# A list scheduler's cost table: undisturbed durations, a shorter distance between engines, and one port that VectorE and GpSimd share

## The chip, the core and the metric

The kernel runs on one core of a Trainium2 chip. The metric is the device time of one execution in microseconds (us). Five engines matter here: TensorE (PE in the profile, with its weight loads as PEld), VectorE (DVE), ScalarE (ACT), GpSimd (POOL), and SyncE (SP), which issues the loads and stores.

## The reference, cut to what matters

One layer of a hybrid block runs over 1024 positions of width 1024, in float32:

```python
h = rmsnorm(x, norm_g)
q, k, v, z_a, u_b, v_b, z_b, g_a, g_b = split(h @ w_in)
y_a = stick_breaking_attention(q, k, v) * silu(z_a)      # 8 heads of 64, causal
y_b = spatial_gating(gelu(u_b), gelu(v_b), ...) * silu(z_b)
merged = sigmoid(g_a) * (y_a @ w_up_a) + sigmoid(g_b) * (y_b @ w_up_b)
out = rmsnorm(x + merged @ w_out, final_norm_g)
```

The attention weight of a key is a sigmoid times a running product over the later keys: a scan along the row.

## The kernel before

**Arithmetic.** Each float32 operand is split into a high part and a low part (`hi_lo`: ScalarE copies the high part, then VectorE or GpSimd subtracts it for the low part), and a product is three matmuls. The input projection runs as 18 groups (`project`), each made of seven products of 12 matmuls of 512 columns, with weight blocks added and subtracted first (Strassen's scheme). Tiles `a` hold raw weights, `b` their split parts, `T` the activations, and `X`, `Y`, `Z` are accumulators in PSUM.

**Attention.** For one block of 128 queries, `attn_row` makes the scores `z` on TensorE, two sigmoids on ScalarE (`keep` in tile `ak`, `beta` in tile `r`), a running product on VectorE (`scan`, line 198, on diagonal blocks; `scan_mult`, line 191, elsewhere), and `beta` times the scan on VectorE or GpSimd. `attn_step` then transposes the weights through TensorE into `tr`, splits them into two tiles `e`, and multiplies them by the values into `o`.

**Who runs what, and when.** Nothing is issued as it is written. Each helper of `Plan` (`mm`, `tt`, `scan`, ...) records a task with its engine, its cost in us, and what it depends on. `Plan.issue` then runs a list schedule: it keeps a clock, and whenever an engine is free it takes the ready task of lowest priority number whose tiles have slots (tiles of one tag are handed out in the order of their first use). A task is ready when its predecessors have ended, plus `LAT` where the predecessor is on another engine, plus 2.0 after a DMA; slots come free `LAT` after their last use. The result is one fixed order of instructions for each engine. On the chip each engine works through its order and waits at each instruction until its inputs are there; so costs and `LAT` change only the order. Which engine runs an operation is fixed in the code.

Priority is the order in which the code was written, except that weight preparation in `project` gets -9000 and groups written under `ahead` get -6000, on all engines but TensorE. TensorE thus takes the oldest work that the plan holds to be ready, and fills in with later products. The task that the plan takes is planned to end like this (line 284):

```python
pick.end = now + pick.cost
busy[eng] = pick.end
```

Planned costs before, for 512 columns: a VectorE `tensor_tensor` 0.841 with both inputs in SBUF and 0.683 with one in PSUM, a GpSimd one 1.530, a scan 1.446, a matmul 0.227.

Of the kernel before, what the change touches and what calls it, by code (L numbers as in the profile page):

```python
# [10 lines left out]
F32 = mybir.dt.float32  # L11
# [9 lines left out]
EPS = 1e-6  # L21
GELU_C = 0.044715
GELU_S = 1.5957691216057308
LAT = 0.7
SCAN = 2.0


class Buf:
# [14 lines left out]
    @property  # L43
    def all(self):
        return View(self, ())
# [38 lines left out]


class Task:
    __slots__ = ("eng", "cost", "fn", "bufs", "deps", "users", "idx", "prio", "tail", "waiting", "ready", "end")


class Plan:  # L90
# [13 lines left out]
    def add(self, eng, cost, fn, out, ins, tail=0.0):  # L104
        t = Task()
        t.eng, t.cost, t.fn, t.tail = eng, cost, fn, tail
        t.idx = len(self.tasks)
        t.prio = t.idx + (self.offset if eng != "PE" else 0)
        t.deps, t.users, t.bufs = set(), [], []
        for v, write in [(v, True) for v in out] + [(v, False) for v in ins]:  # L110
            b = v.buf
            for box, w, other in b.touched:
                if (w or write) and other is not t and all(a < d and c < e for (a, e), (c, d) in zip(box, v.box)):
                    t.deps.add(other)
            b.touched.append((v.box, write, t))
            if b.order is None:
                b.order = self.tag_count.get(b.tag, 0)
                self.tag_count[b.tag] = b.order + 1
            if b not in t.bufs:
                t.bufs.append(b)  # L120
                b.left += 1
        for o in t.deps:
            o.users.append(t)
        self.tasks.append(t)


    def mm(self, out, lhsT, rhs, start, stop, **kw):
        self.add("PE", max(0.109, rhs.n * 0.000417 + 0.0135),
                 lambda: self.nc.tensor.matmul(out.ap(), lhsT=lhsT.ap(), rhs=rhs.ap(), start=start, stop=stop, **kw),  # L129
                 [out], [lhsT, rhs])  # L130

# [30 lines left out]

    def tt(self, out, in0, in1, op, eng="DVE"):
        e = self.nc.vector if eng == "DVE" else self.nc.gpsimd
        near = in0.buf.psum or in1.buf.psum
        cost = out.n * (0.001042 if near else 0.00135) + 0.15 if eng == "DVE" else out.n * 0.00252 + 0.24
        self.add(eng, cost, lambda: e.tensor_tensor(out=out.ap(), in0=in0.ap(), in1=in1.ap(), op=op),  # L167
                 [out], [in0, in1])

# [17 lines left out]
                 [out], [in_])  # L187

    def scan_mult(self, out, in_, init=None):
        self.add("DVE", in_.n * 0.00255 + 0.14,  # L190
                 lambda: self.nc.vector.tensor_tensor_scan(out.ap(), in_.ap(), in_.ap(),  # L191
                                                           1.0 if init is None else init.ap(), op0=ALU.mult,
                                                           op1=ALU.bypass),
                 [out], [in_] + ([] if init is None else [init]))

    def scan(self, out, in_, floor, init):
        self.add("DVE", in_.n * 0.00255 + 0.14,
                 lambda: self.nc.vector.tensor_tensor_scan(out.ap(), in_.ap(), floor.ap(), init, op0=ALU.mult,  # L198
                                                           op1=ALU.max), [out], [in_, floor])

# [31 lines left out]


    def issue(self):
        now, seq = 0.0, 0
        events = []
        ready = {}
        busy = {}
        turn = {}
        free = dict(self.slots)  # L240
        order = []
        for t in self.tasks:
            t.waiting, t.ready = len(t.deps), 0.0
            busy.setdefault(t.eng, 0.0)
            ready.setdefault(t.eng, [])
            if not t.deps:
                heapq.heappush(ready[t.eng], (t.prio, t.idx, t))

        def can_start(t):
            need = {}  # L250
            for b in t.bufs:
                if not b.held:
                    need.setdefault(b.tag, []).append(b.order)
            for tag, orders in need.items():
                nxt = turn.get(tag, 0)
                if free[tag] < len(orders) or sorted(orders) != list(range(nxt, nxt + len(orders))):
                    return False
            return True

        done = 0  # L260
        while done < len(self.tasks):
            started = False
            for eng, heap in ready.items():
                if busy[eng] > now + 1e-9:
                    continue
                skipped = []
                pick = None
                while heap:
                    item = heapq.heappop(heap)
                    if can_start(item[2]):  # L270
                        pick = item[2]
                        break
                    skipped.append(item)
                for item in skipped:
                    heapq.heappush(heap, item)
                if pick is None:
                    continue
                for b in pick.bufs:
                    if not b.held:
                        b.held = True  # L280
                        free[b.tag] -= 1
                        turn[b.tag] = turn.get(b.tag, 0) + 1
                order.append(pick)
                pick.end = now + pick.cost
                busy[eng] = pick.end
                seq += 1
                heapq.heappush(events, (pick.end, seq, 0, pick))
                done += 1
                started = True
            if started:  # L290
                continue
            if not events:
                stuck = [(t.idx, t.eng, [(b.tag, b.order, b.held, turn.get(b.tag, 0), free[b.tag]) for b in t.bufs])
                         for h in ready.values() for _, _, t in sorted(h)[:4]]
                raise RuntimeError(f"no operation can start: {stuck[:12]}")
            now = events[0][0]
            while events and events[0][0] <= now + 1e-9:
                _, _, kind, t = heapq.heappop(events)
                if kind == 1:
                    heapq.heappush(ready[t.eng], (t.prio, t.idx, t))  # L300
                elif kind == 2:
                    free[t] += 1
                elif kind == 0:
                    for u in t.users:
                        lag = t.tail if t.eng == "DMA" else 0.0 if u.eng == t.eng else LAT
                        u.ready = max(u.ready, now + lag)
                        u.waiting -= 1
                        if u.waiting == 0:
                            seq += 1
                            heapq.heappush(events, (max(u.ready, now), seq, 1, u))  # L310
                    for b in t.bufs:
                        b.left -= 1
                        if b.left == 0 and b.tag in free:
                            seq += 1
                            heapq.heappush(events, (now + t.tail + LAT, seq, 2, b.tag))
        self.length = max(t.end for t in self.tasks)
        for t in order:
            ins = t.fn()
            if t.eng != "DMA":
                self.tc.keep_in_program_order(ins)  # L320
# [729 lines left out]
```

## Time and profile before

| what | value |
|---|---|
| time, median of 3 runs | 766.57 us (766.36 to 766.86) |
| the profiled execution: its time, its span | 766.53 us, 764.7 us |
| TensorE busy | 735.0 us (96% of the span), 3524 matmuls |
| VectorE busy | 575.0 us (75%) |
| ScalarE busy | 433.5 us (57%) |
| GpSimd busy | 308.8 us (40%) |
| granted TensorE clock, mean | 0.999 |

Busy time of an engine is the time in which at least one of its instructions was running. Matmuls are pipelined and their ends are modelled, so TensorE counts as busy a little past the point where the next matmul could have started. The span runs from the first to the last instruction; the execution's own time lies 1.8 us above it.

### The profile page before, as it was taken

How to read it: one execution, taken by the hardware profiler on the slowest of the kernel's cores; microseconds unless marked ns; L12 is line 12 of the kernel's file. 1: busy time of each engine (PE TensorE's matmuls, PEld its weight loads, DVE VectorE, ACT ScalarE, POOL GpSimd, SP SyncE). 2: the span in 40 equal slices, each digit the busy share in tenths (PEclk: the TensorE clock that was granted, in tenths of full speed). 3: DMA queues.
4: the chain of work that ended last, by engine and by line, in shares of the span. 5: the costliest groups of instructions: out<-in, count | busy, mean ns of one | idle time of the engine just before them, and what ended most of it. 6: DMA issues, size and time to landing. Idle time of an engine off the chain costs nothing.

```text
span 764.7 us, 10791 instructions
## 1 busy us (share of the span) xinstructions
PE 735.0 (96%) x3524; PEld 606.4 (79%) x3524; DVE 575.0 (75%) x788; ACT 433.5 (57%) x920; POOL 308.8 (40%) x298
## 2 busy tenths in 40 slices
PE   4989999999889999999999999999999999999996
PEld 3877788888777888887888888878888887888885
DVE  4868754688899787898999988897998878841122
ACT  6636474756756755666757676676867433411122
POOL 1500637497666576274345538234140300013110
PEclk9999999999999999999999999999999999999999
DMA  9412494424344375454543656354597677760022
GB/s 338 176 64 96 144 255 159 146 96 138 113 127 127 103 212 185 141 166 137 153 124 114 191 165 180 108 137 127 173 311 255 213 237 231 252 228 1 29 82 111
DMA packets 69177, 121.31 MB, mean 159 GB/s; under 512 B 7296, under 2 KB 17024, under 8 KB 69120
## 3 DMA queue, kind: packets, MB, share of 16 engines
q1 hardware_dynamic: 67968, 118.52, 49.3%
q10 hardware_dynamic: 1152, 2.10, 0.7%
q8 instruction: 28, 0.46, 0.3%
q14 instruction: 29, 0.24, 0.1%
HBM read 81.27 MB, written 39.32 MB: 158 GB/s over the span
## 4 chain that ended last, share of the span: by engine, by line
PE 83%; DVE 9%; issue 3%; DMA 2%; ACT 2%; POOL 1%; SPq 0%; POOLq 0%; DVEq 0%; ACTq 0%
PE Y L129 22%; PE X L129 21%; PE Z L129 18%; PE z L129 9%; PE o L129 8%; PE tr L133 5%; DVE b L167 2%; DVE ak L198 1%; DVE ak L191 1%; DMA k<-in_x_dram 1%; DVE e L167 1%; DMA k<-d 1%; DVE T L167 1%; DVE f L167 1%; DVE r L167 1%
## 5 line engine op out<-in xcount | busy, mean ns | idle before, releaser
L129 PE MATMUL Y<-T,b 128*128 128x512 f32 x672 | 180.0, 398 | 1.6 <-ACT b L157 1.3
L129 PE MATMUL X<-T,b 128*128 128x512 f32 x660 | 177.9, 398 | 0.0
L129 PE MATMUL Z<-T,b 128*128 128x512 f32 x540 | 145.2, 397 | 0.0
L129 PEld LDWEIGHTS Y<-T,b 128*128 128x128 f32 x672 | 122.3, 188 | 26.0 <-ACT b L157 1.7
L157 ACT CAST b<-a 128x512 fp32r<-128x512 f32 (+1 forms) x152 | 93.6, 617 | 81.9 <-PE Y L129 22.5
L129 PEld LDWEIGHTS X<-T,b 128*128 128x128 f32 x660 | 119.8, 188 | 22.8 <-POOL b L167 0.4
L167 DVE TENSOR_TENSOR b<-a,b 128x512 fp32r<-128x512 f32 (+1 forms) x112 | 99.4, 889 | 28.8 <-ACT b L157 20.0
L129 PEld LDWEIGHTS Z<-T,b 128*128 128x128 f32 x540 | 98.1, 188 | 18.3
L167 POOL TENSOR_TENSOR b<-a,b 128x512 fp32r<-128x512 f32 x40 | 60.7, 1516 | 119.8 <-ACT b L157 106.6
L198 DVE TENSOR_TENSOR_SCAN ak<-ak,c 128x128 f32<-128x128 f32 (+1 forms) x64 | 72.8, 1141 | 3.5 <-ACT ak L146 3.4
L167 POOL TENSOR_TENSOR a<-a,a 128x512 f32<-128x512 f32 x40 | 61.5, 1537 | 28.9 <-DVE b L167 15.3
L167 POOL TENSOR_TENSOR f<-f,f 128x512 f32<-128x512 f32 (+1 forms) x38 | 56.2, 1484 | 36.0 <-ACT f L146 14.7
L157 ACT CAST e<-tr 128x512 fp32r<-128x512 f32 (+1 forms) x96 | 45.7, 480 | 36.5 <-PE tr L133 33.3
L167 POOL TENSOR_TENSOR r<-r,ak 128x512 f32<-128x512 f32 x32 | 46.9, 1474 | 39.4 <-DVE ak L191 33.4
L133 PE MATMUL tr<-c,r 128*128 128x128 f32 x320 | 58.5, 273 | 2.6 <-DVE r L167 2.5
L129 PE MATMUL o<-e,k 128*128 128x512 f32 (+1 forms) x192 | 57.6, 343 | 3.3 <-DVE e L167 3.2
L146 ACT ACTIVATE ak<-z 128x128 f32<-128x128 f32 (+2 forms) x96 | 47.4, 494 | 20.4 <-PE z L129 18.1
L129 PE MATMUL z<-k,k 128*128 128x512 f32 (+2 forms) x216 | 56.8, 352 | 0.9 <-DMA k<-d 0.9
L167 DVE TENSOR_TENSOR e<-tr,e 128x512 fp32r<-128x512 f32 (+1 forms) x96 | 52.0, 545 | 7.3 <-ACT e L157 6.4
L146 ACT ACTIVATE r<-z 128x128 f32<-128x128 f32 (+2 forms) x96 | 46.9, 495 | 13.1 <-PE tr L133 12.5
L133 PEld LDWEIGHTS tr<-c,r 128*128 128x128 f32 x320 | 39.9, 140 | 13.6 <-DVE r L167 3.4
L191 DVE TENSOR_TENSOR_SCAN ak<-ak,c 128x512 f32<-128x512 f32 x32 | 50.5, 1588 | 0.2
(217 smaller groups left out, 1148.5 us busy)
## 6 DMA issues: line engine op xcount, KB each, us to landing
d<-f SPq DMA_DIRECT2D x112, 256.0 KB, 2.8
a<-in_w_pairs_dram SPq DMA_DIRECT2D x80, 256.0 KB, 2.8
f<-d SPq DMA_DIRECT2D x72, 256.0 KB, 3.2
k<-d SPq DMA_DIRECT2D x48, 256.0 KB, 4.8
k<-in_x_dram SPq DMA_DIRECT2D x8, 512.0 KB, 7.2
d<-b SPq DMA_DIRECT2D x16, 256.0 KB, 2.3
k<-d SPq DMA_DIRECT2D x8, 512.0 KB, 6.3
a<-in_w_up_dram SPq DMA_DIRECT2D x16, 256.0 KB, 4.3
```

Source lines behind the costliest of these rows:

```text
L129: lambda: self.nc.tensor.matmul(out.ap(), lhsT=lhsT.ap(), rhs=rhs.ap(), start=start, stop=stop, **kw),
L133: self.add("PE", 0.109, lambda: self.nc.tensor.transpose(out=out.ap(), in_=in_.ap(), identity=ident.ap()), [out], [in_, ident])
L146: return self.nc.scalar.activation(out=out.ap(), in_=in_.ap(), func=func, scale=sc, **kw)
L157: lambda: self.nc.scalar.copy(out=out.ap(), in_=in_.ap()), [out], [in_])
L167: self.add(eng, cost, lambda: e.tensor_tensor(out=out.ap(), in0=in0.ap(), in1=in1.ap(), op=op), [out], [in0, in1])
L191: lambda: self.nc.vector.tensor_tensor_scan(out.ap(), in_.ap(), in_.ap(), 1.0 if init is None else init.ap(), op0=ALU.mult, op1=ALU.bypass),
L198: lambda: self.nc.vector.tensor_tensor_scan(out.ap(), in_.ap(), floor.ap(), init, op0=ALU.mult, op1=ALU.max), [out], [in_, floor])
```

## The change

Four things in the cost table and one in the scheduler:

- `LAT`, the distance that the plan puts between engines and before a slot is reused, goes from 0.7 to 0.25 us.
- `tensor_tensor` costs go to 0.673 (VectorE) and 1.289 (GpSimd) for 512 columns, whatever memory the inputs lie in; scans go to 1.225.
- A matmul whose moving operand is float32 (not the rounded `float32r`) counts twice.
- A task of VectorE or GpSimd with more than one input view that is wider than 64 and lies in SBUF is marked `shared`. In the plan, shared tasks of both engines pass one port one after the other: a shared task ends at the later of now and the port's last end, plus its cost, and its engine is held until then.

```diff
-LAT = 0.7
+LAT = 0.25
...
+        t.shared = eng in ("DVE", "POOL") and len([v for v in ins if v.n > 64 and not v.buf.psum]) > 1
...
-        self.add("PE", max(0.109, rhs.n * 0.000417 + 0.0135),
+        self.add("PE", max(0.109, rhs.n * 0.000417 + 0.0135) * (2 if rhs.buf.dt == F32 else 1),
...
-        near = in0.buf.psum or in1.buf.psum
-        cost = out.n * (0.001042 if near else 0.00135) + 0.15 if eng == "DVE" else out.n * 0.00252 + 0.24
+        cost = out.n * 0.001042 + 0.14 if eng == "DVE" else out.n * 0.0024 + 0.06
...
-        self.add("DVE", in_.n * 0.00255 + 0.14,
+        self.add("DVE", in_.n * 0.0021 + 0.15,
...
-        now, seq = 0.0, 0
+        now, seq, port = 0.0, 0, 0.0
...
                 pick.end = now + pick.cost
+                if pick.shared:
+
+                    pick.end = port = max(now, port) + pick.cost
                 busy[eng] = pick.end
```

The scan's new cost stands in both `scan_mult` and `scan`. No instruction, tile, engine or buffer count is changed.

## Rows read from the trace of the kernel before

**Rows 1.** The page, part 1: busy time, share of span, instructions.
```profile
PE 735.0 (96%) x3524; PEld 606.4 (79%) x3524; DVE 575.0 (75%) x788; ACT 433.5 (57%) x920; POOL 308.8 (40%) x298
```
**Rows 2.** By stretch: length; PE, PEld, DVE, ACT, POOL busy; clock; DMA share, GB/s.
```profile
0.00:20.00 20.00, 8.83 (x32) 7.00 (x33) 9.92 (x19) 12.48 (x22) 3.07 (x12) 1.00 0.94 342
20.00:140.00 120.00, 116.40 (x529) 94.71 (x528) 80.10 (x122) 67.78 (x134) 47.00 (x39) 1.00 0.50 152
140.00:200.00 60.00, 60.00 (x296) 50.19 (x295) 47.17 (x66) 39.83 (x72) 41.49 (x34) 1.00 0.35 115
200.00:240.00 40.00, 35.27 (x167) 28.00 (x167) 39.30 (x44) 26.44 (x63) 29.28 (x24) 1.00 0.39 123
240.00:620.00 380.00, 377.52 (x1878) 312.68 (x1877) 333.15 (x435) 246.85 (x553) 169.70 (x167) 1.00 0.55 168
```
**Rows 3.** Waits of TensorE's matmuls, 140 to 620: total, times, longest.
```profile
PE o L129 <- DVE e L167: 3.2, 4, 1.5
PE tr L133 <- DVE r L167: 2.5, 2, 1.5
PE z L129 <- DMA k<-d: 0.9, 2, 0.7
PE o L129 <- DVE os L167: 0.5, 1, 0.5
```
**Rows 4.** Waits of TensorE's weight loads, 140 to 620.
```profile
PEld o L129 <- DVE e L167: 5.5, 6, 1.9
PEld tr L133 <- DVE r L167: 3.4, 2, 2.0
```
**Rows 5.** VectorE and GpSimd by tile: ns minimum/median/maximum, first and last start.
```profile
L167 DVE TENSOR_TENSOR b<-a,b x112: 410/687/1779, 70.2 to 597.6; 128x512 fp32r<-128x512 f32 x108, 128x256 fp32r<-128x256 f32 x4
L167 DVE TENSOR_TENSOR f<-Z,f x30: 659/692/694, 88.4 to 670.9; 128x512 f32<-128x512 f32 x30
L167 POOL TENSOR_TENSOR b<-a,b x40: 1284/1348/2321, 77.5 to 553.6; 128x512 fp32r<-128x512 f32 x40
L191 DVE TENSOR_TENSOR_SCAN ak<-ak,c x32: 1252/1339/2307, 231.8 to 611.3; 128x512 f32<-128x512 f32 x32
L167 DVE TENSOR_TENSOR r<-r,s x8: 682/1616/1791, 159.3 to 294.6; 128x512 f32<-128x512 f32 x8
```
**Rows 6.** Groups by line and shape: busy us, mean ns, idle before.
```profile
L191 DVE TENSOR_TENSOR_SCAN ak<-ak,c 128x512 f32<-128x512 f32 x32 | 50.5, 1588 | 0.2
L167 DVE TENSOR_TENSOR r<-r,s 128x512 f32<-128x512 f32 x8 | 11.8, 1478 | 0.3 <-POOL s L167 0.2
```
**Rows 7.** In order of time, near 347: start, length, instruction, idle before.
```profile
345.93 1.73 DVE L167 TENSOR_TENSOR b<-a,b 128x512 fp32r<-128x512 f32 x1
347.07 1.75 POOL L167 TENSOR_TENSOR b<-a,b 128x512 fp32r<-128x512 f32 x1
347.70 1.67 DVE L167 TENSOR_TENSOR a<-a,a 128x512 f32<-128x512 f32 x1
349.29 0.28 DVE L167 TENSOR_TENSOR e<-tr,e 128x128 fp32r<-128x128 f32 x1
349.62 0.33 PE L129 MATMUL o<-e,k 128*128 128x128 f32 x1 [0.83 <-DVE e L167]
```
**Rows 8.** In order of time, near 82.
```profile
82.30 1.98 PE L129 MATMUL Y<-T,b 128*128 128x512 f32 x8
82.50 0.59 ACT L157 CAST f<-X 128x512 fp32r<-128x512 f32 x1 [1.42 <-PE X L129]
```
**Rows 9.** In order of time, the start.
```profile
7.38 1.97 PE L133 MATMUL tr<-c,k 128*128 128x128 f32 x8 [7.38 <-DVE k L173]
9.19 1.06 ACT L146 ACTIVATE ak<-k 128x1024 bf16<-128x1024 f32 x1 [3.91 <-DMA k<-in_x_dram]
10.25 0.57 ACT L157 CAST T<-tr 128x512 fp32r<-128x512 f32 x1
14.05 1.16 ACT L157 CAST T<-a 128x512 fp32r<-128x512 f32 x2
```

More of the change, by code (lines that the diff above doesn't have):

```diff
@@ L86 @@
 class Task:
-    __slots__ = ("eng", "cost", "fn", "bufs", "deps", "users", "idx", "prio", "tail", "waiting", "ready", "end")
+    __slots__ = ("eng", "cost", "fn", "bufs", "deps", "users", "idx", "prio", "tail", "waiting", "ready", "end",
+                 "shared")
 class Plan:
@@ L196, in scan @@
     def scan(self, out, in_, floor, init):
-        self.add("DVE", in_.n * 0.00255 + 0.14,
+        self.add("DVE", in_.n * 0.0021 + 0.15,
                  lambda: self.nc.vector.tensor_tensor_scan(out.ap(), in_.ap(), floor.ap(), init, op0=ALU.mult,
```

## The prediction

> **What bounds the kernel now.** I read the page's busy times first. TensorE is busy for 735.0 of 764.7 us [rows 1], and the change adds and removes no instruction, so its work is the floor. All that another order can win lies in the 29.7 us in which TensorE is idle.
>
> The busy times by stretch say where those are [rows 2]. 11.2 us fall in the first 20 us (20.00 - 8.83), before and while the first blocks arrive; 3.6 between 20 and 140; none between 140 and 200; 4.73 in the forty microseconds from 200 to 240; 2.48 in the long stretch from 240 to 620; the other 7.7 after 620, most of them at the very end, where little choice of order is left. So the middle, 140 to 620, in which projections and attention are interleaved, holds 4.73 + 2.48 = 7.2 us. The reader is to see in the row of 200 to 240 that VectorE is busy for 39.30 of 40 us there: attention has begun, and TensorE waits for VectorE.
>
> The waits of TensorE's matmuls name the same thing: of 7.1 us between 140 and 620, 3.2 are waits of `o` for the low part `e`, 2.5 waits of a transpose for the weights `r`, 0.5 waits of `o` for an earlier output, and only 0.9 a DMA [rows 3]. VectorE ends 6.2 us of them. The weight loads, each of which counts as busy for a shorter time, give 5.5 + 3.4 = 8.9 us for the two large ones, against 5.7 by the matmuls [rows 4]. The true loss is between these.
>
> Why VectorE is late is seen in the durations [rows 5]. Its subtraction `b<-a,b`, both inputs in SBUF, takes 687 ns at the median and up to 1779; the same operation with one input in PSUM, `f<-Z,f`, never takes more than 694. GpSimd's takes 1284 at best and 2321 at worst. The timeline shows it at work [rows 7]: a VectorE subtraction of 1.73 us, a GpSimd one of 1.75 that overlaps it, a VectorE one of 1.67, each held by the other; behind them stands the 0.28 us `e` that TensorE has been waiting 0.83 us for. The two engines take turns, and the later one loses up to a whole operation of the other. The plan of before knows nothing of this: it charges 0.841 each time, right for the mean and wrong for nearly every single one, so the order it writes for TensorE puts attention steps where their inputs are not yet there.
>
> **The change, part by part.** The time is summed against the profiled execution's own 766.53 us, which is 0.04 below the median.
>
> *Durations and the port.* The new costs, 0.673 and 1.289, are the undisturbed ones (687 and 1284 ns [rows 5]), and the port adds the turn-taking where the plan sees it come. In the plan, then, a `z`, a transpose or an `o` becomes ready when it really does, and TensorE gets a product of `X`, `Y` or `Z` before it instead. Such products are at hand: weight preparation has the lowest priority numbers and runs ahead by several `b` tiles. What this can return is bounded by rows. At the low end it is 0: between 200 and 240 VectorE is busy 98% of the time, and if that is its own need, no order shortens it. At the high end it is the 6.2 us of waits for VectorE, or 9.4 (8.9 + 0.5) as the weight loads have it. I take half of the 6.2, so **-3.1 us**: in 240 to 620 VectorE is busy only 333 of 380 us, and the waits there are errors of order; in 200 to 240 part of the load is its own.
>
> *The shorter distance.* It costs no instruction, so its price is in order alone. Is 0.25 us true? After a matmul, ScalarE starts its copy at 82.50 where the next group's first matmul started at 82.30, so 0.20 us after the plan's end of the product [rows 8]. After VectorE, TensorE starts 0.05 us after the end (349.29 + 0.28 to 349.62) [rows 7]. So the new distance still lies above what the chip shows, where the old one lay 0.5 above. But this surplus was slack: an attention row passes from TensorE over ScalarE and VectorE back to TensorE, and loses 0.45 us of it per step. I cost it at **0** for the middle, because the named slack was needed against the blocks that the plan now counts; if the counting is wrong, the slack is missed (second rival). The shorter hold of slots is covered by the same argument.
>
> *The start.* Here a step moves, and I follow it through the plan's rules by hand, for the order alone. The second input block's square stands in ScalarE's order ahead of the first copy out of `tr`: it waits 3.91 us for the block's DMA until 9.19, and the copy comes at 10.25 [rows 9], though the transposes had begun at 7.38, eight of them taking 1.97. With four steps between engines each 0.45 us shorter, the plan has the first `tr` ready just before that block (7.55 against 7.92 on the plan's clock), so the copy goes first. On the chip it could then run at about 8.4. But the second and later copies still stand behind squares that wait for blocks; the first weights' copy at 14.05 ends this chain, and it can gain between 0 and one square (1.06). I take **-0.4**. Of the queues, SP's alone carries loads, and its order there keeps the order of the code; POOL's small operations behind the squares move with them.
>
> *Edits without effect.* The factor of two for float32 matmuls meets none: the moving operand of every `mm` (`T`, `e`, `kh`, `wv`, `ws`, `ys`, `wo`) is made as `float32r`, and transposes have their own cost. Nothing hides this; it is nothing.
>
> *What the port does not see.* `scan_mult` passes one wide view, since its two inputs are the same, and `wide(r)` in `r<-r,s` is 8 columns broadcast to 512; so neither is marked. Yet the rows show both held up: the scan at line 191 takes 1252 at best, 2307 at worst and 1588 on average, the product `r<-r,s` 682 at best and 1478 on average [rows 5, 6]. The plan charges 1.225 and 0.673. It thus lacks 32 x 0.363 + 8 x 0.805 = 18.1 us of VectorE time between 159 and 613; the old plan, charging 1.446 and 0.841, lacked 32 x 0.142 + 8 x 0.637 = 9.6. VectorE has 333 busy of 380 us there, so most of this is taken up by idle time; for the sum I leave it at 0, with a third of the 18.1, 6 us, as the other end. The Trainium skill, page "SBUF — State Buffer", section "Who interferes with whom", says that a VectorE instruction with two SBUF inputs contends with a GpSimd one that reads SBUF, and makes no exception for twice the same tile; by that rule the mark in this change is incomplete. The trace agrees: line 191 goes up to 2307 ns.
>
> The sum: 766.53 - 3.1 - 0.4 = **763.0 us**.
>
> **The rivals.**
>
> *Nothing reaches the end: 766.5.* The port itself is the limit where TensorE idles, and a better plan of a full queue is still a full queue. For it: 39.30 of 40 us [rows 2]. Waits move to other instructions and come to the same 7.2. Against it: after 240 VectorE has 12% to spare and TensorE still waits.
>
> *Slower: 769.* The unmarked operations, with the slack gone. Place: attention rows off the diagonal (line 191) and the normalisation (`r<-r,s`), 159 to 613. There the plan has VectorE ready too early by 18.1 us in all, and TensorE, in order, stands at a transpose or an `o` meanwhile. If a third reaches TensorE, the time is 766.5 - 3.5 + 6 = 769.0; if half, 772. It decides from 3.5 / 18.1, a fifth. For it: line 191 is 0.363 us over its planned cost on average. Against it: line 191 feeds GpSimd's product first, which is planned with the port, and TensorE mostly has products in between.
>
> *Much faster: 756 to 759.* All waits for VectorE go, as the weight loads count them, and the start gains a whole square: 766.5 - 9.4 - 1.06 = 756.1; with the matmuls' own count, 766.5 - 6.2 - 1.06 = 759.3. For it: between 140 and 200, with much GpSimd and VectorE work but before the first scans, TensorE has no idle time [rows 2]. Against it: the unmarked 18.1 us.
>
> **How the numbers follow.** The forecast (759.5 to 765.0) has 0.42, much faster 0.15, no change 0.20, slower 0.23. What this kernel's measurement can tell from no change is about 0.2%, or 1.5 us: below 765.0 is faster, above 768.1 slower. So faster is 0.57, same 0.20, slower 0.23. The range of 757.5 to 769.5 leaves out some 0.08 of the much faster end (unmarked blocks all harmless) and some 0.10 beyond the slower rival's first value. The forecast's own range is 759.5 to 765.0.
>
> **What will show it.** Right: between 200 and 240 TensorE is busy over 37 of 40 us, and its waits for `e` and `r` between 140 and 620 fall below 3.5 us, while its busy time stays at 735 or so. The maxima of `b<-a,b` stay near 1.78 us, since blocking is planned for, not removed. The copy out of `tr` comes before 9.19 at the start, and the first weights' copy before 14.05. Wrong: new waits of transposes behind line 191 or of `o` behind `e`, in the stretches after 240 (the slower rival); the same idle time between 200 and 240 with VectorE still at 98% (no change); or a gap near the end, should attention run out before the groups that fill its pauses.

## The result and the profile after

The changed kernel takes **785.23 us** (median of 4 runs, 784.01 to 786.99), the kernel before 766.70 beside it: **1.0244 times as long [1.0221, 1.0267]**, slower by 18.5 us. The forecast was 763.0, with a range that ended at 769.5. The profiled execution took 784.3 us with a span of 782.5, 17.8 above that of before.

The page's part 1 after, in the columns of [rows 1] (its span is 782.5 us):

```profile
PE 744.9 (95%) x3524; PEld 611.5 (78%) x3524; DVE 575.1 (73%) x788; ACT 433.3 (55%) x920; POOL 303.7 (39%) x298
```

The work of VectorE and ScalarE is the same to 0.2 us. TensorE, with the same 3524 matmuls, is busy 9.9 us longer; its mean granted clock is 0.987 in this execution, 0.999 before. By stretch, in the columns of [rows 2]:

```profile
0.00:20.00 20.00, 9.77 (x38) 7.73 (x39) 10.64 (x19) 12.05 (x22) 3.20 (x12) 1.00 0.91 328
20.00:140.00 120.00, 114.84 (x521) 93.73 (x521) 78.88 (x121) 68.31 (x136) 47.83 (x39) 1.00 0.48 151
140.00:200.00 60.00, 59.02 (x282) 48.68 (x282) 49.92 (x64) 37.52 (x68) 37.81 (x29) 1.00 0.34 113
200.00:240.00 40.00, 39.38 (x187) 32.52 (x186) 30.31 (x33) 20.94 (x45) 26.12 (x25) 1.00 0.41 140
240.00:260.00 20.00, 15.06 (x51) 10.87 (x50) 17.75 (x26) 13.79 (x34) 8.68 (x6) 0.67 0.33 85
260.00:640.00 380.00, 370.90 (x1832) 305.04 (x1832) 322.68 (x421) 241.45 (x542) 161.82 (x163) 1.00 0.53 161
```

Here it is better to count matmuls than busy time, since a matmul at a lower clock is busy longer for the same work. Before, 1878 of them ran in the 380 us from 240 to 620 [rows 2], one in 0.2023 us, 98.8 in 20 us. Against that rate, and stretch by stretch, after has 6 more before 20, 8 fewer from 20 to 140, 14 fewer from 140 to 200, 20 more from 200 to 240, 48 fewer from 240 to 260, and 46 fewer (1878 - 1832) in the 380 us from 260 to 640. Together some 90 matmuls are missing, 90 x 0.2023 = 18.2 us: about the whole difference of the spans, 17.8. The count is rough for single stretches, since it puts a transpose of 128 columns beside a product of 512: of the 51 in the gap 23 are transposes, so the work missing there is more than 48 mean matmuls, and the 14 fewer from 140 to 200, with 0.98 us of idle time, are in the main larger ones. So the forty microseconds that the prediction looked at did improve (idle 4.73 us before, 0.62 now), and the next twenty lost more than twice as much.

What TensorE does in those twenty is in the timeline (start, length, instruction, idle time before and what ended it):

```profile
240.03 0.40 PE L131 MATMUL Z<-T,b 128*128 128x512 f32 x1
242.09 0.50 PE L131 MATMUL o<-e,k 128*128 128x512 f32 x1 [1.24 <-ACT e L159]
243.77 1.11 PE L131 MATMUL o<-e,k 128*128 128x512 f32 x2 [1.18 <-DVE e L168]
246.59 1.48 PE L131 MATMUL z<-k,k 128*128 128x512 f32 x3
254.58 0.60 ACT L148 ACTIVATE r<-Y 128x512 f32<-128x512 f32 x1 [0.78 <-PE tr L135]
258.85 1.48 PE L131 MATMUL Y<-T,b 128*128 128x512 f32 x3
```

Between the last `Z` of one group at 240.03 and the first `Y` of the next at 258.85, its order holds attention alone: scores, transposes, outputs. Such a step goes round four engines, and with nothing else in the order TensorE waits out each round. The next group could not start its product because the accumulator `Y` was still held: the second spatial-gating group, `make_vb(1)`, reads its first quadrant out of `Y` into a tile `r` (254.58), slots of `r` are handed out in the order of first use, and the rows of the first head, `head(0, 0)`, are written before it and so come first. The scans show how late that head is. Its first scan stood at 203.1 before, and its first scan off the diagonal (line 191 before, 192 after) at 231.8 [rows 5]; they stand at 217.4 and 248.2 now, 14 and 16 us later, and the product behind them waits for attention's tiles:

```profile
L198 DVE TENSOR_TENSOR_SCAN ak<-ak,c x64: 409/972/2317, 203.1 to 598.4; 128x128 f32<-128x128 f32 x16, 128x256 f32<-128x256 f32 x16, 128x384 f32<-128x384 f32 x16, 128x512 f32<-128x512 f32 x16
L199 DVE TENSOR_TENSOR_SCAN ak<-ak,c x64: 405/1018/2308, 217.4 to 610.6; 128x128 f32<-128x128 f32 x16, 128x256 f32<-128x256 f32 x16, 128x384 f32<-128x384 f32 x16, 128x512 f32<-128x512 f32 x16
L192 DVE TENSOR_TENSOR_SCAN ak<-ak,c x32: 1257/1338/2417, 248.2 to 624.8; 128x512 f32<-128x512 f32 x32
```

The granted clock is lower there too. In the 20 us row it is 0.67; in five-microsecond stretches:

```profile
240.00:245.00 5.00, 2.58 (x9) 1.33 (x7) 4.86 (x9) 3.33 (x10) 1.30 (x2) 0.82 0.15 52
245.00:250.00 5.00, 5.00 (x20) 4.14 (x19) 4.50 (x8) 4.08 (x10) 0.34 (x1) 0.50 0.00 0
```

After two idle stretches of 1.24 and 1.18 us stands a fully busy row at 0.50, the lower level of 1.2 GHz, with 20 matmuls in 5 us. A part of TensorE's longer busy time is here.

The waits of TensorE's matmuls in the long stretch after the gap, 260 to 640, answer to [rows 3]:

```profile
PE z L131 <- DMA k<-d: 3.7, 3, 2.3
PE tr L135 <- POOL r L168: 2.0, 4, 1.0
```

There the waits for VectorE that the prediction wanted to shorten are nearly gone, and yet 46 matmuls are missing; the largest wait is now for a transfer of `k` (0.9 us in all before), the next one for the weights `r` that GpSimd multiplies.

### The profile page after: what moved, and what is told of

The parts are those of the page before. It is cut to its first block, busy times and chain, and to the rows that moved or that the text cites. A ratio compares the mean times of both kernels' runs of the same rounds, so it can differ in the third digit from the quotient of the medians.

```text
span 782.5 us, 10778 instructions
## 1 busy us (share of the span) xinstructions
PE 744.9 (95%) x3524; PEld 611.5 (78%) x3524; DVE 575.1 (73%) x788; ACT 433.3 (55%) x920; POOL 303.7 (39%) x298
## 4 chain that ended last, share of the span: by engine, by line
PE 73%; DMA 7%; DVE 7%; POOL 6%; issue 4%; ACT 2%; SPq 1%; POOLq 0%; DVEq 0%; ACTq 0%
PE Y L131 19%; PE X L131 17%; PE Z L131 15%; PE z L131 9%; PE o L131 8%; PE tr L135 4%; POOL r L168 3%; DMA f<-d 2%; DMA d<-f 2%; DVE r L168 1%; POOL b L168 1%; DVE b L168 1%; DMA k<-in_x_dram 1%; DVE f L168 1%; POOL a L168 1%
## 5 line engine op out<-in xcount | busy, mean ns | idle before, releaser
L131 PE MATMUL Y<-T,b 128*128 128x512 f32 x672 | 182.5, 402 | 3.5 <-ACT b L159 1.6
L131 PE MATMUL X<-T,b 128*128 128x512 f32 x660 | 174.2, 396 | 0.0
L131 PEld LDWEIGHTS X<-T,b 128*128 128x128 f32 x660 | 120.9, 188 | 22.7
L168 DVE TENSOR_TENSOR b<-a,b 128x512 fp32r<-128x512 f32 (+1 forms) x112 | 97.3, 870 | 42.3 <-ACT b L159 32.4
L168 POOL TENSOR_TENSOR b<-a,b 128x512 fp32r<-128x512 f32 x40 | 58.2, 1456 | 115.5 <-ACT b L159 99.1
L199 DVE TENSOR_TENSOR_SCAN ak<-ak,c 128x128 f32<-128x128 f32 (+1 forms) x64 | 69.5, 1091 | 0.3 <-ACT ak L148 0.2
L131 PE MATMUL o<-e,k 128*128 128x512 f32 (+1 forms) x192 | 63.5, 365 | 5.4 <-DVE e L168 2.5
L135 PE MATMUL tr<-c,r 128*128 128x128 f32 x320 | 63.0, 283 | 4.4 <-POOL r L168 3.3
L131 PE MATMUL z<-k,k 128*128 128x512 f32 (+2 forms) x216 | 60.7, 367 | 4.3 <-DMA k<-d 3.7
L135 PEld LDWEIGHTS tr<-c,r 128*128 128x128 f32 x320 | 42.6, 144 | 19.1 <-POOL r L168 6.6
L131 PEld LDWEIGHTS o<-e,k 128*128 128x128 f32 x192 | 37.7, 198 | 16.4 <-DVE e L168 4.9
```

Of the source, the lines that this page charges most:

```text
L135: self.add("PE", 0.109, lambda: self.nc.tensor.transpose(out=out.ap(), in_=in_.ap(), identity=ident.ap()), [out], [in_, ident])
```

## The experiments

Three theories stood at first. In the expectations, **theory 1** is that the port is the cause: a plan that serialises VectorE and GpSimd writes an order with a gap in it. **Theory 2** is that the shorter distance is the cause: 0.45 us of slack per step was needed, and without it TensorE stands at many small waits. **Theory 3** is that any new order moves the time by 1% or more, with no pattern. All ratios are to the kernel before, on the same chip. "The distance" is `LAT`.

### The four parts by themselves

**lat_only**: the kernel before with the short distance alone.

```diff
-LAT = 0.7
+LAT = 0.25
```

> The kernel before with the shorter distance alone (0.25 us), old costs, no port. Theory 1, the port: the 20 us with 51 matmuls come from the port in the plan, which makes attention's operations late there and lets projections run ahead; then this kernel has no such gap and takes 762 to 770 us. Theory 2, the lost slack: the shorter distance takes away what covered the blocks; then most of the loss is here, 778 us or more, as many small waits of transposes and of o. Theory 3, any new order: the time moves by 1% or more either way with no pattern over the four kernels.

**costs_only**: the changed kernel with the old distance and no port, so the new costs alone (with the factor for float32, which meets no matmul).

```diff
-LAT = 0.25
+LAT = 0.7
...
-                if pick.shared:
+                if False and pick.shared:
```

> The new costs alone: distance 0.7 us, no port. Theory 1: no long gap, 764 to 770 us. Theory 2: the slack is kept, so near the kernel before, 764 to 770 us too; it differs from theory 1 by what the next kernel does. Theory 3: anywhere from 760 to 785 us.

**no_port**: the changed kernel without the port.

```diff
-                if pick.shared:
+                if False and pick.shared:
```

> The changed kernel without the port: distance 0.25 us and new costs. Theory 1: the gap near 240 to 260 is gone and the time comes back to 765 to 772 us, with some small waits left because blocking is no longer counted. Theory 2: still slow, 778 us or more, since the distance is still 0.25 and costs are at their lowest. Theory 3: anywhere.

**port_lat70**: the changed kernel with the old distance.

```diff
-LAT = 0.25
+LAT = 0.7
```

> The changed kernel with the distance back at 0.7 us: new costs and the port. Theory 1: still slow, 780 us or more, since the longer distance makes the port's waits longer still in the plan and the gap stays. Theory 2: the slack is back, so 762 to 770 us. Theory 3: anywhere.

| kernel | distance | costs | port | us | ratio | plan's length | span |
|---|---|---|---|---|---|---|---|
| before | 0.7 | old | no | 767.12 | 1 | 758.0 | 764.7 |
| lat_only | 0.25 | old | no | 791.09 | 1.0316 [1.0301, 1.0332] | 757.2 | 788.6 |
| costs_only | 0.7 | new | no | 776.28 | 1.0128 [1.0113, 1.0143] | 754.3 | 774.3 |
| no_port | 0.25 | new | no | 807.91 | 1.0537 [1.0520, 1.0555] | 745.0 | 805.7 |
| port_lat70 | 0.7 | new | yes | 782.21 | 1.0202 [1.0186, 1.0217] | 779.9 | 780.2 |
| after | 0.25 | new | yes | 785.23 | 1.0244 [1.0221, 1.0267] | 760.5 | 782.5 |

The row of after is the result above, measured beside 766.70. The span is that of the profiled execution.

Every part makes the kernel slower by itself, and they don't add. The distance costs 24.0 us with the old costs (791.09 - 767.12), 31.6 with the new ones and no port (807.91 - 776.28), and only 3.0 with the port (785.23 - 782.21). The new costs alone take 9.2 us. The port takes 5.9 us more at the old distance, and *gives back* 22.7 at the short one (807.91 - 785.23). costs_only, which theories 1 and 2 both put at 764 to 770 us, missed both.

The plan's length is `Plan.issue`'s own (`self.length`): the end of its last task on its own clock. It is no measurement but follows from each kernel's code, and the order of matmuls that comes with it is the one in the trace. Set beside the span, it parts two losses. port_lat70's plan is 21.9 us longer than that of before, and the chip keeps to it (780.2 for 779.9): that loss is planned. no_port's plan is 13.0 us shorter, and the chip takes 60.7 us longer than the plan: that loss is the missing margin. The changed kernel has some of both. With the port, the short distance takes 19.4 us off the plan (779.9 to 760.5), and the chip returns none of it. Theory 3 does not fit: what the chip adds to the plan goes with the margin, 0.3 us with port and old distance, 6.7 before, 20.0 in costs_only, 22.0 after, 31.4 in lat_only, 60.7 with neither port nor old distance.

The traces show the two kinds. Without the port it is, in the main, many small waits. TensorE's, 140 to 640, lat_only:

```profile
PE o L129 <- DVE e L167: 9.7, 12, 2.1
PE o L129 <- ACT e L157: 7.5, 5, 3.5
PE tr L133 <- DVE r L167: 2.9, 5, 0.8
```

The same view of costs_only:

```profile
PE o L131 <- DVE e L168: 5.9, 9, 1.2
```

And of no_port:

```profile
PE o L131 <- DVE e L168: 23.0, 27, 1.8
PE o L131 <- ACT e L159: 5.9, 6, 2.3
PE tr L135 <- DVE r L168: 4.8, 7, 1.3
```

It is the wait of [rows 3], `o` for `e`, four times before, nine with costs_only, 12 with lat_only and 27 with both: each step towards a more hopeful plan puts more `o` where their `e` isn't there yet. (The view also counts the `o` of the gating groups, which reads a tile `b`; attention's alone, `o<-e,k`, are 4, 7, 8 and 21.)

But lat_only has a long gap too, without the port. From 280 to 300 TensorE gets through 53 matmuls, 46 below the mean rate, some 9.3 of the 24.0 us; the longest wait in it is not attention's but the second gating group's:

```profile
280.00:300.00 20.00, 13.17 (x53) 9.71 (x52) 14.92 (x19) 8.99 (x16) 15.45 (x13) 0.79 0.53 175
292.45 0.58 PE L129 MATMUL o<-e,b 128*128 128x256 f32 x1 [3.53 <-ACT e L157]
```

This gap is in the plan: lat_only's plan leaves TensorE idle for 10.4 of the 40 us from 260 to 300, that of before for none.

With the port the loss is a few long stretches. port_lat70 by stretch:

```profile
160.00:200.00 40.00, 34.56 (x164) 27.98 (x163) 31.45 (x40) 19.18 (x38) 27.87 (x26) 0.91 0.33 105
240.00:280.00 40.00, 34.88 (x154) 27.76 (x153) 32.08 (x39) 22.79 (x47) 21.63 (x15) 0.87 0.27 81
```

Against 198 matmuls in 40 us, the first row lacks 34 and the second 44: 78 x 0.2023 = 15.8 us, about the whole of its 15.1 us. Its plan holds both: TensorE is planned for 31.6 of the 40 us from 160 to 200, and for 26.2 of those from 240 to 280. The two gaps are of different kinds. In the second, attention is alone, as in the changed kernel. The first lies before any attention (the first scan is at 196.6); its longest wait is the first gating group's:

```profile
180.39 0.58 PE L131 MATMUL o<-e,b 128*128 128x256 f32 x1 [3.69 <-ACT e L159]
```

So both theories hold in the main, each in its own place: theory 1 for what the change does with the port, theory 2 for the distance without it.

### Where the distance matters

**margin_into_pe**: the kernel before, with 0.25 everywhere but where TensorE is the one that waits.

```diff
-    lag = t.tail if t.eng == "DMA" else 0.0 if u.eng == t.eng else LAT
+    lag = t.tail if t.eng == "DMA" else 0.0 if u.eng == t.eng else 0.7 if u.eng == "PE" else 0.25
...
-    heapq.heappush(events, (now + t.tail + LAT, seq, 2, b.tag))
+    heapq.heappush(events, (now + t.tail + 0.25, seq, 2, b.tag))
```

> The kernel before (old costs, no port) with the distance at 0.25 us everywhere, for slots too, but 0.7 us where TensorE is the one that waits. Theory 4: the distance is a margin for the bottleneck alone; TensorE must not be sent to an attention step early, the other engines may. Then this returns most of the 24 us that 0.25 us everywhere cost: 766 to 772 us, with TensorE's waits for e at some 4 us. Theory 5: each engine works in order, so a ScalarE or VectorE instruction that is sent early holds up those behind it, and the margin counts on every hop: 780 us or more.

779.91 us, 1.0163 [1.0133, 1.0193]: of lat_only's 3.16% about half comes back. That is far from theory 4's 766 to 772 and at the edge of theory 5's 780. The margin that counts is not only the one on the last step into TensorE; the rest must lie in the steps among the other engines, through which TensorE is reached, and in the slots, which the next run prices. Its waits, 140 to 640, are spread over every producer:

```profile
PE o L129 <- ACT e L157: 4.1, 3, 2.5
PE tr L133 <- DVE r L167: 3.0, 4, 1.3
PE tr L133 <- POOL r L167: 2.3, 2, 1.9
PE o L129 <- DVE e L167: 2.3, 4, 1.0
```

**slots_only**: the kernel before, with 0.25 for the release of slots alone (the second pair of lines above).

```diff
-    heapq.heappush(events, (now + t.tail + LAT, seq, 2, b.tag))
+    heapq.heappush(events, (now + t.tail + 0.25, seq, 2, b.tag))
```

> The kernel before with only the slots' release at 0.25 us after the last use, the distance between engines still 0.7. Theories 4 and 5 both: slots are freed by semaphores as fast as data, so little changes: 764 to 770 us. If the shorter hold of slots is what hurt, 778 us or more.

769.82 us, 1.0034 [1.0015, 1.0052]. As both theories had it, the release of slots matters little: by itself it costs 2.6 us.

### What the slack is slack against

**no_reads** puts a constant fill in the place of GpSimd's wide operations with two inputs, in the order of before, so that GpSimd reads nothing wide from SBUF; **no_reads_lat25** does the same in the order of lat_only.

```diff
+        if eng == "POOL" and out.n > 64:
+            o = out.f32() if out.buf.dt == F32R else out
+            self.add(eng, cost, lambda: e.memset(o.ap(), 0.5), [out], [in0, in1])
+            return
```

> The kernel before, in its own order, but each of GpSimd's wide tensor_tensor is replaced by a memset of the same output (the values computed are left out; it reads nothing, so VectorE should not be held up). VectorE's b<-a,b should then stay at 0.69 us throughout. Theory 6: TensorE's waits for VectorE come from the blocks; they all but vanish, 755 to 762 us. Theory 7: they come from the order itself; 763 us or more.

> The same replacement in the kernel with the distance alone at 0.25 us, which took 24 us longer than before. Theory 6: the margin of 0.7 us covers the blocks, and without blocks 0.25 us is enough: within 6 us of the run with the same replacement and 0.7 us. Theory 7: the margin covers other errors of the plan; still 15 us or more behind it.

756.86 us, 0.9863 [0.9842, 0.9884], and 764.27 us, 0.9959 [0.9945, 0.9972]. no_reads by tile:

```profile
L171 DVE TENSOR_TENSOR b<-a,b x112: 420/691/695, 70.0 to 587.8; 128x512 fp32r<-128x512 f32 x108, 128x256 fp32r<-128x256 f32 x4
L169 POOL MEMSET b<- x40: 519/527/530, 73.2 to 542.6; 128x512 f32 x40
L195 DVE TENSOR_TENSOR_SCAN ak<-ak,c x32: 1259/1276/1285, 224.5 to 601.5; 128x512 f32<-128x512 f32 x32
```

The longest `b<-a,b` falls from 1779 ns [rows 5] to 695 and the longest scan from 2307 to 1285, so nearly all of the variation in these durations was GpSimd's reading. No order was changed, and TensorE's idle time in 200 to 240 is gone:

```profile
200.00:240.00 40.00, 40.00 (x200) 33.33 (x199) 31.02 (x52) 29.13 (x69) 9.93 (x25) 1.00 0.48 148
```

This answers a question that [rows 2] left open: of VectorE's 39.30 us there, at least 8 were waiting and not need, since more instructions (52 for 44) now take 31.02. Without GpSimd's reads, the short distance costs 7.4 us in place of 24.0. Some 16.6 of the 24 us were therefore the blocks; the recorded expectations had set within 6 and 15 or more as the two answers, and the result lies between, nearer to the blocks. The 7.4 have one place, the planned gap of lat_only's order, which no_reads_lat25 shares. By stretch:

```profile
260.00:300.00 40.00, 34.44 (x161) 28.01 (x160) 25.17 (x42) 19.42 (x41) 10.13 (x23) 0.87 0.56 181
```

37 of 198 matmuls are missing in this row, 37 x 0.2023 = 7.5 us. Without blocks the chip keeps near the plan at either distance: spans of 754.8 and 762.4 us for plans of 758.0 and 757.2. One reservation on the 16.6: a fill takes 527 ns where the subtraction took 1284 or more [rows 5], so GpSimd itself is also less late, and they hold that as well.

The Trainium skill, page "SBUF — State Buffer", section "Who interferes with whom", says that GpSimd instructions which only write SBUF do not contend with VectorE's second input. These two runs agree: with fills in the place of GpSimd's wide operations, no subtraction `b<-a,b` took above 695 ns.

### A fuller port

**marked_all**: the changed kernel, with the operations marked too that the prediction found unmarked, the wide scan and `r<-r,s`.

```diff
+        self.tasks[-1].shared = True
...
             pl.tt(t3, t3, wide(r), ALU.mult)
+            pl.tasks[-1].shared = True
```

> The changed kernel with the two unmarked operations marked as shared as well (the scan with the same tile twice, and the product with a column broadcast). Rival of the prediction, unmarked operations: the waits after 260 are theirs, so TensorE's idle time from 260 to 640 falls from 9 us to 4 or less, and the time goes to 780 us or below, unless the plan itself puts a new gap in. Theory 1 turned round, the plan's own gaps: a fuller port delays attention further in the plan, more idle time is planned, and the time rises to 788 us or more with one or two long gaps.

801.82 us, 1.0447 [1.0423, 1.0471]: a plan that knows more of the blocks is some 16 us slower still, and the plan itself is 783.0 us long, 22.5 longer than that of the changed kernel. The rows by stretch show a second gap of the first one's kind:

```profile
240.00:260.00 20.00, 12.95 (x48) 8.50 (x49) 17.91 (x26) 12.94 (x34) 9.21 (x6) 0.79 0.33 86
640.00:660.00 20.00, 13.54 (x51) 8.35 (x51) 19.69 (x28) 11.65 (x32) 7.79 (x5) 0.78 0.06 19
```

VectorE is busy for 17.91 and 19.69 of 20 us in them. The slower rival, that the unmarked operations are the price, is not borne out: to mark them returns nothing. In the changed kernel itself, 260 to 640, TensorE waits for no `r` of VectorE's and for 2.0 us of GpSimd's, which is made from the scan; even if all of it were the scan's, it is a small part of 18.5 us.

### The gap itself

**free_accumulator**: the changed kernel, with the second gating group's first quadrant copied out of PSUM into a tile `f2`, whose slots don't stand behind the head's.

```diff
-        after(0, 0, xx.all, True)
+        if g == VB[1]:
+            c11 = buf("f2")
+            pl.copy(c11.all, xx.all)
+            after(0, 0, c11.all, False)
+        else:
+            after(0, 0, xx.all, True)
```

> The changed kernel with one ScalarE copy more: in the second spatial-gating group the first quadrant is copied out of PSUM, so that its accumulator is free without a tile r. If the gap of 240 to 260 is there because the next group's first product waits for this accumulator, which waits for attention's turn in r, the products of Y come before 250 and the gap there goes; the time falls to 770 to 775 us if nothing else holds them, or stays at 783 to 790 us with the gap moved to the next place where attention has to be finished. If the accumulator is not the cause, the gap stays at 240 to 260.

789.57 us, 1.0282 [1.0253, 1.0310]. By stretch:

```profile
240.00:260.00 20.00, 20.00 (x99) 16.52 (x98) 14.68 (x23) 12.77 (x33) 6.68 (x6) 1.00 0.30 88
260.00:300.00 40.00, 29.07 (x111) 21.40 (x110) 30.05 (x41) 22.05 (x42) 24.02 (x19) 0.74 0.37 110
```

The gap leaves 240 to 260 (99 matmuls in place of 51) and stands from 260 to 300, where 87 of 198 are missing. The held accumulator was what ended the products at 240, as read; it was not the cause of the loss. Products spent earlier are missing later: as read, attention, which is late, still has its rows to go round.

**head_first_lat70** and **head_first_lat25** act on that, in port_lat70 and in the changed kernel. They change three priorities at once: the first head's rows go ahead of all weight preparation, the first gating group's weight preparation goes back to its place in the code, and so does the second `u` group, which ran ahead.

```diff
+        self.pe_offset = 0
-        t.prio = t.idx + (self.offset if eng != "PE" else 0)
+        t.prio = t.idx + (self.offset if eng != "PE" else self.pe_offset)
...
+        prep = 0 if g == VB[0] else -9000
-        use_at, pl.offset = pl.offset, -9000
+        use_at, pl.offset = pl.offset, prep
...
-            pl.offset = -9000
+            pl.offset = prep
...
+    pl.offset, pl.pe_offset = -9500, -800
     head(0, 0)
-    ahead(make_u, 1)
+    pl.offset = pl.pe_offset = 0
+    make_u(1)
```

> New costs, the port and the distance of 0.7 us (782.2 us as it stood), with three priorities changed: the first attention head ahead of all weight preparation, the first spatial-gating group's preparation and the second u group at their place in the code. Theory 1 turned round: the loss with port and 0.7 us is idle time that the plan itself holds where attention begins; if attention starts first, the plan holds 17 us less of it, and the chip follows the plan: 763 to 767 us. If the chip does not follow, 775 us or more.

> The same three priorities in the changed kernel (distance 0.25 us). The gap of 240 to 260 goes or shrinks to half, and the many small waits stay, since the margin is still short: 775 to 783 us. If the small waits were a consequence of the late start too, 770 us or less.

772.28 us, 1.0061 [1.0043, 1.0080], where port_lat70 had 782.21; and 777.07 us, 1.0136 [1.0113, 1.0159], where the changed kernel has 785.23. By stretch, head_first_lat70:

```profile
160.00:200.00 40.00, 38.35 (x194) 31.79 (x193) 33.73 (x45) 23.56 (x45) 28.00 (x25) 1.00 0.35 112
200.00:240.00 40.00, 36.97 (x182) 29.40 (x182) 38.17 (x49) 27.66 (x64) 24.43 (x20) 1.00 0.35 102
240.00:280.00 40.00, 40.00 (x195) 33.23 (x194) 34.15 (x44) 25.51 (x46) 29.86 (x23) 1.00 0.52 157
```

And head_first_lat25:

```profile
200.00:240.00 40.00, 37.02 (x174) 30.02 (x173) 33.89 (x47) 26.27 (x61) 20.40 (x16) 0.91 0.28 82
240.00:260.00 20.00, 20.00 (x93) 16.54 (x93) 13.04 (x19) 13.36 (x23) 13.77 (x12) 1.00 0.55 174
260.00:640.00 380.00, 371.53 (x1831) 306.15 (x1830) 322.53 (x418) 236.64 (x534) 164.11 (x162) 1.00 0.54 165
```

The long gaps are gone in head_first_lat70, and in head_first_lat25 the one from 240 to 260; there a shorter one remains from 200 to 240, with 174 matmuls and a clock of 0.91. The first scan off the diagonal now stands at 213.8 and 209.8. That gives back about 10 and 8 us. So these priorities make the gaps. Which of the three does it was not separated: the lateness of the first head fits the gap from 240 on, and the first gap of port_lat70, before attention, can't be its work. Between 260 and 640, head_first_lat25 has 1831 matmuls where the changed kernel has 1832: taking the gap away returned nothing there. The first result is between its two recorded answers (763 to 767, or 775 and more), the second as expected. No version with the port, the new costs or the short distance was faster than before.

## Why the prediction was wrong, by its steps

**Durations and the port, forecast -3.1: the step that failed, and by most.** At the old distance these parts cost 15.1 us (782.21 against 767.12), 9.2 by the costs and 5.9 by the port. The reading of the loss was right: the waits were blocks, a plan that counts them moves TensorE's waits elsewhere, and in 200 to 240 TensorE is busy for 39.38 us where over 37 was foretold. What failed is the cover, "such products are at hand", and with it the floor of 0: a new order can lose. With the port the plan has less of VectorE and GpSimd to hand out, and the first head gets through its rows later, whatever the distance: its first scan off the diagonal stands at 231.8 before, 248.2 after and 248.3 in port_lat70, and without the port at 224.3 in no_port.

```profile
L192 DVE TENSOR_TENSOR_SCAN ak<-ak,c x32: 1253/1277/2243, 248.3 to 634.1; 128x512 f32<-128x512 f32 x32
```

So products are spent early, and at 240 attention stands alone. The gain of 4.1 us came, and 9.7 us (48 matmuls) went in the next 20. That weight preparation at -9000 takes VectorE and GpSimd first is read from the priorities and not shown by itself. All this could be had before the run: the plan of the changed kernel has TensorE at work for 10.8 of the 20 us from 240 to 260, that of before for all 20. The prediction followed the plan's rules by hand at the start alone and argued for the middle.

**The shorter distance, forecast 0: the second error.** Beside the port, as the prediction priced it, it costs 3.0 us; by itself 24.0. It was priced at 0 on the argument that the slack was needed against blocks which the plan now counts. The runs support the first half (without GpSimd's reads 7.4 us in place of 24.0, and those 7.4 in one planned gap) and the second in part (3.0 us with the port, 31.6 without). Yet the 19.4 us that the short distance takes off the plan with the port never reach the chip. The 0.20 and 0.05 us of distance [rows 7, 8] said only what an undisturbed step takes. The prediction set no other end to this term, although it named the 0.45 us that each step loses.

**Port and distance together.** At the old distance the port is a loss of 5.9 us, at the short one a gain of 22.7. It works as a substitute for slack and is the poorer one. Slack lets the order absorb any delay; the port moves only those that the plan foresees, and pays in planned idle time (754.3 us of plan without it, 779.9 with it, at the old distance). The new costs alone cost 9.2 us: the old 0.841 had been slack of another kind. The prediction calls it right for the mean; the mean of the subtraction was 0.887, so it lay 46 ns too low, and the new 0.673 lies 214 ns too low:

```profile
L167 DVE TENSOR_TENSOR b<-a,b 128x512 fp32r<-128x512 f32 x108 | 95.7, 887 | 26.3 <-ACT b L157 17.5 <-PE Z L129 3.7 <-POOL b L167 3.2
```

**The start, forecast -0.4: right, and mis-sized.** In order of time, as [rows 9]:

```profile
8.38 0.58 ACT L159 CAST T<-tr 128x512 fp32r<-128x512 f32 x1 [3.22 <-PE tr L135]
8.97 1.06 ACT L148 ACTIVATE ak<-k 128x1024 bf16<-128x1024 f32 x1
13.13 1.14 ACT L159 CAST T<-a 128x512 fp32r<-128x512 f32 x2
```

The copy goes ahead of the square, at the 8.4 foretold, and the weights' copy comes 0.92 us earlier (14.05 to 13.13), near the other end of 1.06. TensorE's idle time in the first 20 us falls from 11.17 to 10.23. But from 20 to 140 it rises from 3.60 to 5.16, so by 140 the gain is gone; the prediction took it as kept to the end.

**Maxima of `b<-a,b`: right.** They stay, since blocks are planned for and not removed:

```profile
L168 DVE TENSOR_TENSOR b<-a,b x112: 410/691/1828, 70.2 to 617.4; 128x512 fp32r<-128x512 f32 x108, 128x256 fp32r<-128x256 f32 x4
```

**The unmarked operations, forecast 0: the slower rival's mechanism was not the price.** That rival got the side right (slower), by luck: marked_all returned nothing, and the waits that could be theirs come to 2.0 us from 260 to 640. The factor for float32 was not run by itself; no matmul in the changed kernel's plan is charged twice, so it had nothing to change.

**The other signs.** Waits for `e` and `r` below 3.5 us between 140 and 620: right for what VectorE makes, the reading of [rows 3] (2.5 us, all of `e` and all in the gap), and wrong for all makers, since 1.2 us for ScalarE's `e` and 3.3 for GpSimd's `r` have come in. TensorE's busy time did not stay at 735. "A gap, should attention run out" was listed for the end; it came where attention begins, and what ran out was the products.

**What stays open.** With the gaps gone and the old distance, head_first_lat70 is still 0.6% over before; its plan is 763.3 us long, 5.3 over that of before, which is about all of it, but which of the new costs and the port holds this was not separated. Nor were the 46 matmuls between 260 and 640 traced to a single wait: the ones shown add up to less.

## What to carry to other kernels

In a static schedule a margin that measurement calls too long can be the only thing that absorbs variation which the plan doesn't model; before it is cut, price it by the variation (here maxima of 1.1 us over the median) and not by the undisturbed distance (0.20 us). A truer model can make the plan's length truer and not shorter (779.9 us planned, 780.2 on the chip, with the port and the old distance): where it makes a resource scarce, look at what the priorities starve first, and whether the work that fills the pauses is then still there. A term that is only "another order" has no floor at zero. And a static plan can be read before the run: its own length and its own idle stretches on the engine that bounds the kernel say which part of a change is planned loss.

## What the runs showed of the hardware that was not expected

- Two pauses of 1.24 and 1.18 us in TensorE's work, about 240 to 244, were followed by a row of 5 us with TensorE busy throughout and a granted clock of 0.50 (1.2 GHz). By the count above, the gap of 20 us (240 to 260) cost 48 matmuls, 9.7 us, while its idle time was only 4.94.
- VectorE's scan, whose two inputs are the same tile, is held up by GpSimd's reads like the other operations with two inputs in SBUF, as the prediction read from maxima; taking the reads away shows it: at most 2307 ns before, 1285 with GpSimd filling only.
- GpSimd's fill of 512 columns takes 527 ns, and 40 of them delayed no `b<-a,b` beyond 695 ns.
